# A fourth pair of seven products in the down projections of a two-layer decoder trunk, with own pages for sums of weights, an earlier table load and separate statistics tiles

## The chip, the cores and the metric

One core of one Trainium2 chip runs the whole kernel in one launch. The metric is the device time of that core in microseconds (us). Before the change the median of three runs was 2143.47 us (2143.34 to 2143.54).

## The reference

Input is x (256 tokens of 2048 features, float32) with the weights. Each sublayer is `h = h + RMSNorm_post(f(RMSNorm_pre(h)))`.

```python
def short_conv_mixer(u, w_in, conv_w, w_out):
    proj = u @ w_in
    xin, gate_c, gate_b = jnp.split(proj, 3, axis=-1)
...
    return (gate_b * conv) @ w_out
...
def sq_relu_mlp(u, w_up, w_down):
    return jnp.square(jax.nn.relu(u @ w_up)) @ w_down
```

Layer 0 is a gated convolution of width 3 over tokens and an MLP with 8192 hidden features. Then keys and values for layer 1 come from the normed h. Layer 1 is stick-breaking attention with 16 heads of 128, and again an MLP. Nearly all arithmetic is in the weight products: 2048 x 6144, 2048 x 2048, two MLPs of 2048 x 8192 and 8192 x 2048, keys and values 2048 x 4096, queries and output 2048 x 2048 each.

## The kernel before

**Split operands.** Every weight and every activation is split into a high part (rounded to the float32r format) and a low part (the rest), and a product is the sum of high x high, high x low and low x high. So one *product* (`product`, line 557) is three matmuls of 128 x 128 by 512 columns into one PSUM bank. ScalarE (ACT) makes the high part of a page of weights as a copy (line 389 in `act`), VectorE (DVE) the low part as a subtraction (line 397 in `tt`), both in `split` (line 487). TensorE (PE) multiplies.

**Groups.** A `Group` computes 256 tokens by 1024 columns from 2048 rows of weights, in sixteen chunks of 128 rows; a chunk of weights is a 512 KB page of 128 x 1024. For each chunk there are four products: two token blocks b by two column halves c, into four PSUM banks `acc`. Each MLP runs in four quarters q of 2048 hidden features. A quarter is two up groups (j = 0, 1), whose results go through relu, transpose and square into the operands `hid`, and two down groups, which read `hid` and gather into `part` pages. There are eight quarters in all.

**Pairs of seven.** Two chunks form a pair, that is a 2 x 2 block product with eight products. For the pairs in `UP_SEVEN` and `DN_SEVEN` (line 316, both pairs 0, 1 and 2) the method `seven` (line 610) uses seven products in place of eight, by Winograd's scheme: four sums of weight quarters t1 to t4 (DVE, 512 columns each), and sums of the activations, made once per pair and quarter by `make_forms` (line 529). Products go to three of the `acc` banks and to four banks q of the other set. `combine` (line 678) joins those four with DVE operations, and `finals` (line 688) adds them to the `acc` banks at the end of the group. The first up group of each layer and the last down group of each layer have no pairs of seven. `turns` (line 711) sets the sequence of the pairs: 3, 0, 4, 1, 5, 2, 6, 7 with the three pairs of seven between the others.

A seven takes three pages of class `raw` (two loaded, one for the sums t1 and t2) and one of `r2` (t4), and four pages each of `hi` and `lo`, the last one half used. t3 overwrites a quarter of the second raw page.

**The planner.** Nothing is ordered by hand on the engines. The code records tasks, and `Plan.place` (line 162) lays them out beforehand: each task has an engine, an estimated duration, a due time derived from the tasks that need it, and pages from pools of fixed size (`SLOTS`, line 29). An engine then runs its list strictly in that sequence. PE runs the products in the recorded sequence, with transposes and attention matmuls as side tasks between them. Loads go out on SyncE's queue (SP) once a raw page is free.

**Start.** ACT issues the load of the gains, then takes its first table together with the first split of x (`enter`, line 949). In the lead stage six PSUM banks are filled while x and the input weights arrive. A mean over features is a matmul with a matrix of 1/2048 (`mean`, line 344; `statistics`, line 964).

**Norms.** `Norms.post` (line 788) squares a finished bank on ACT with a running sum into one column of the tile `stats` (line 352, shared by all norms), multiplies by the gain on DVE (`mg`), and after the fourth quarter of columns adds up, takes the root on ACT and the reciprocal on DVE, and adds to h (`hh`). At four places the last group of a run ends in parts, so that this work begins earlier (`run` with `leave`, line 747): block 0 column half by column half, then block 1 with both halves together.

## Time and profile before

| | |
|---|---|
| median of 3 runs | 2143.47 us |
| profiled execution | 2144.19 us, span 2142.5 us |
| PE | 2121.9 us busy, 9942 matmuls |
| DVE | 1725.9 us, 2325 instructions |
| ACT | 1283.8 us, 1787 instructions |
| read from HBM | 417.40 MB, 199 GB/s over the span |
| a full MLP quarter | 169.52 us (up groups 43.28 each, down groups 41.48 each) |

The profile is of one execution. A row of the timeline gives start, length, engine, line, operation, written and read tiles, the count of merged instructions and, in brackets, how long the engine stood idle before and what released it. Lengths of following instructions on one engine may overlap. In the names, h and l before a letter are high and low part, r the raw page, and u, d, in the stage (up, down, input); a page of a pair of seven carries layer, quarter, group, pair and a letter: rd0201c is layer 0, quarter 2, down group 0, pair 1, page c, which holds the sums t1 and t2. Line numbers are those of the kernel before; in the changed one they are shifted by one in the helpers.

### The profile page before, as it was taken

What the parts mean: (1) busy time and instruction counts of PE and PEld (TensorE: products, weight loads), DVE (VectorE), ACT (ScalarE), POOL (GpSimd) and SP (SyncE); (2) the same over time, 40 slices, a digit from 0 to 9 for tenths busy, and PEclk for the clock granted to TensorE, in tenths of its full rate; (3) what the DMA queues carried; (4) which work ended last, traced back from release to release, by engine and by line L of the source; (5) the groups of instructions that cost most, each with busy time, mean ns of one, the idle gap of its engine ahead of it and who ended that gap; (6) DMA issues with size and microseconds to landing.
All of it is one profiled execution on the core that took longest, in us unless ns stands there. A gap on an engine that the chain in (4) does not pass through costs nothing.

```text
span 2142.5 us, 27458 instructions
## 1 busy us (share of the span) xinstructions
PE 2121.9 (99%) x9942; PEld 1773.0 (83%) x9942; DVE 1725.9 (81%) x2325; ACT 1283.8 (60%) x1787; POOL 1.0 (0%) x7
## 2 busy tenths in 40 slices
PE   8999999999999999999999999999999999999998
PEld 7888888788888888888888888888788888888886
DVE  7766656898999899899656777558988998999995
ACT  6444445765575566566557776547655665665663
POOL 0000000000000000000000000000000000000000
PEclk9999999999999999999999999999999999999999
DMA  8656666456556656667664446655566466656672
GB/s 314 186 189 187 208 226 205 158 197 207 195 178 219 204 175 207 216 198 264 221 207 151 158 158 198 228 190 191 171 217 205 165 222 208 195 196 201 189 277 103
DMA packets 118648, 427.59 MB, mean 200 GB/s; under 512 B 13168, under 2 KB 13296, under 8 KB 118512
## 3 DMA queue, kind: packets, MB, share of 16 engines
q1 hardware_dynamic: 118368, 425.77, 59.9%
q8 instruction: 78, 1.28, 0.2%
q14 instruction: 58, 0.48, 0.1%
q10 hardware_dynamic: 144, 0.07, 0.0%
HBM read 417.40 MB, written 8.39 MB: 199 GB/s over the span
## 4 chain that ended last, share of the span: by engine, by line
PE 99%; ACT 0%; DVE 0%; DMA 0%; issue 0%; DVEq 0%; ACTq 0%
PE acc L560 72%; PE acc L436 11%; PE q L560 11%; PE tr L443 2%; PE lead L436 2%; PE z L1193 0%; PE o L1243 0%; PE ex L1223 0%; PE o L1244 0%; PE z L1194 0%; DMA x<-xT 0%; ACT hid L389 0%; ACT hu L389 0%; DVE hh L404 0%; PE ey L1228 0%
## 5 line engine op out<-in xcount | busy, mean ns | idle before, releaser
L560 PE MATMUL acc<-hu,u 128*128 128x512 f32 x1376 | 439.7, 391 | 0.0
L560 PE MATMUL acc<-hd,hid 128*128 128x512 f32 x1376 | 435.4, 390 | 0.0
L560 PEld LDWEIGHTS acc<-hd,hid 128*128 128x128 f32 x1376 | 258.4, 188 | 53.0
L560 PEld LDWEIGHTS acc<-hu,u 128*128 128x128 f32 x1376 | 258.3, 188 | 52.7
L560 PE MATMUL acc<-lu,u 128*128 128x512 f32 x688 | 267.8, 389 | 0.0
L560 PE MATMUL acc<-ld,hid 128*128 128x512 f32 x688 | 267.8, 389 | 0.0
L397 DVE TENSOR_TENSOR ld<-rd,hd 128x1024 fp32r<-128x1024 f32 x172 | 208.1, 1222 | 51.3 <-ACT hd L389 49.7
L397 DVE TENSOR_TENSOR lu<-ru,hu 128x1024 fp32r<-128x1024 f32 x172 | 208.4, 1222 | 42.6 <-ACT hu L389 41.4
L389 ACT ACTIVATE hd<-rd 128x1024 fp32r<-128x1024 f32 x172 | 180.1, 1057 | 101.9 <-PE acc L560 73.8
L389 ACT ACTIVATE hu<-ru 128x1024 fp32r<-128x1024 f32 x172 | 178.8, 1059 | 84.3 <-PE acc L560 55.1
L397 DVE TENSOR_TENSOR lin<-rin,hin 128x1024 fp32r<-128x1024 f32 (+1 forms) x102 | 117.6, 1162 | 68.6 <-ACT hin L389 66.4
L389 ACT ACTIVATE hin<-rin 128x1024 fp32r<-128x1024 f32 (+1 forms) x102 | 102.0, 1009 | 116.5 <-PE acc L436 75.7
L436 PE MATMUL acc<-u,hin 128*128 128x512 f32 x672 | 168.5, 393 | 0.0
L560 PEld LDWEIGHTS acc<-ld,hid 128*128 128x128 f32 x688 | 129.2, 188 | 26.2
L560 PEld LDWEIGHTS acc<-lu,u 128*128 128x128 f32 x688 | 129.3, 188 | 25.9
L436 PEld LDWEIGHTS acc<-u,hin 128*128 128x128 f32 x672 | 120.9, 189 | 21.7
L436 PEld LDWEIGHTS acc<-u,lin 128*128 128x128 f32 x672 | 91.7, 190 | 6.6
L436 PE MATMUL acc<-u,lin 128*128 128x256 f32 x672 | 93.7, 282 | 0.0
L560 PE MATMUL acc<-hk,u 128*128 128x512 f32 x256 | 86.0, 398 | 0.0
L560 PE MATMUL acc<-hv,u 128*128 128x512 f32 x256 | 82.8, 394 | 0.0
L560 PE MATMUL acc<-hq,u 128*128 128x512 f32 x256 | 81.7, 393 | 0.0
L397 DVE TENSOR_TENSOR q<-q,q 128x512 f32<-128x512 f32 x112 | 76.8, 686 | 4.6
(3165 smaller groups left out, 4140.2 us busy)
## 6 DMA issues: line engine op xcount, KB each, us to landing
ru<-w_up SPq DMA_DIRECT2D x172, 512.0 KB, 3.8
rd<-w_dn SPq DMA_DIRECT2D x172, 512.0 KB, 4.4
rin<-w_in SPq DMA_DIRECT2D x94, 512.0 KB, 3.6
ro<-w_out SPq DMA_DIRECT2D x32, 512.0 KB, 3.5
rv<-w_v SPq DMA_DIRECT2D x32, 512.0 KB, 3.9
rk<-w_k SPq DMA_DIRECT2D x32, 512.0 KB, 4.4
rq<-w_q SPq DMA_DIRECT2D x32, 512.0 KB, 3.8
rwo<-w_wo SPq DMA_DIRECT2D x32, 512.0 KB, 3.5
```

What stands on the lines that cost most here:

```text
L389: nc.scalar.activation(out_.w(), in_.r(), func, scale=val(scale), **more)
L397: "DVE", dve(width(out_)), lambda: nc.vector.tensor_tensor(out_.w(), a.r(), b.r(), op=op),
L436: lambda: nc.tensor.matmul(out_.w(), lhsT.w(), rhs.w(), start=start, stop=stop, skip_group_check=skip),
L443: nc.tensor.matmul(to.w(), src.r(), ident.tile[:], is_transpose=True, start=j == 0, stop=True, skip_group_check=True)
L560: nc.tensor.matmul(ps.w(), a.w(), w.w(), start=first and j == 0, stop=last and j == 2, skip_group_check=skip)
```

## The change

`DN_SEVEN` gains pair 4, so each of the fourteen down groups with pairs of seven does four pairs with seven products and four with eight; `turns` then gives the sequence 3, 0, 5, 1, 2, 4, 6, 7. The page of t1 and t2 has its own class `rt`. The pools become 6 raw, 2 rt, 2 r2, 6 hi, 5 lo, 8 x8, 8 x4 and 12 c2. The planner now counts a read of a PSUM bank by another engine as something to wait for, and takes 0.08 us (DVE) or 0.09 us (ACT) off between following operations of an engine. ACT's table for the root is asked for as a task of its own at the start. `mean` is replaced by `ones` with the scale 1/2048 in the root. Every statistic has its own tile. The last groups of a run end half by half in both blocks. A branch that would make sums by DMA is rewritten, but stays unused (`SUMS_BY_DMA` is empty).

```diff
-SLOTS = {"raw": 8, "r2": 2, "hi": 6, "lo": 6, "x8": 8, "x4": 6, "c2": 14}
+SLOTS = {"raw": 6, "rt": 2, "r2": 2, "hi": 6, "lo": 5, "x8": 8, "x4": 8, "c2": 12}
...
+    OVERLAP = {"DVE": 0.08, "ACT": 0.09}
...
+            if b.bank is not None:
+                t.preds.update(w for a, z, w in b.reads if w.eng != eng and any(a < q and p < z for p, q in v.spans))
...
-                avail[e] = t.end
+                avail[e] = t.end - (self.OVERLAP.get(e, 0.0) if dur > 0.2 else 0.0)
...
-DN_SEVEN = (0, 1, 2)
+DN_SEVEN = (0, 1, 2, 4)
...
     def small(n=1):
-        a = used[0]
-        used[0] += n
-        return stats.col(a, a + n)
+        used[0] += 1
+        b = home([P, n], F32, f"stat{used[0]}")
+        b.home, b.owner = False, True
+        return b.col()
...
+    plan.task("ACT", 0.05, lambda: None, table=TABLES[AF.Sqrt])
...
-            r0, r1, r2 = [raw_page(f"r{self.name}{j}{z}") for z in "abc"]
-            r3 = page("r2", [P, HALF], F32, f"r{self.name}{j}d")
-            load(r0.col(), w[base], own=(r0, r1, r2))
+            r0, r2 = raw_page(f"r{name}a"), page("rt", [P, CW], F32, f"r{name}c")
...
+                r1 = raw_page(f"r{name}b")
+                r3 = page("r2", [P, HALF], F32, f"r{name}d")
+                load(r0.col(), w[base])
...
-            for c in range(2):
-                for i in range(gr.n - EDGE, gr.n):
-                    gr.half(0, c, i, i == gr.n - 1)
-                gr.finish(0, c)
-            for i in range(gr.n - EDGE, gr.n):
-                gr.unit(1, i, i == gr.n - 1)
-            for c in range(2):
-                gr.finish(1, c)
+            for b in range(NB):
+                for c in range(2):
+                    for i in range(gr.n - EDGE, gr.n):
+                        gr.half(b, c, i, i == gr.n - 1)
+                    gr.finish(b, c)
...
-            self.ss = [small(4) for _ in range(NB)]
+            self.ss = [[small() for _ in range(4)] for _ in range(NB)]
...
-            mm(ps.col(0, T), mean.col(), acc.col(0, T), 0.44)
-            act(rstd, ps.col(0, T), AF.Sqrt, bias=eps.col())
+            mm(ps.col(0, T), ones.col(), acc.col(0, T), 0.44)
+            act(rstd, ps.col(0, T), AF.Sqrt, bias=eps.col(), scale=1.0 / D)
```

What the planner makes of it is seen at three places. On DVE in layer 0, quarter 2, first down group, before the change (rd, hd and ld are raw, high and low pages of the down weights; 0201 and 0202 with a letter are pairs 1 and 2 of this group, 02010 and 02011 its chunks 10 and 11, which are pair 5, of eight; the number behind the underscore only tells buffers apart):

```order
L397 TENSOR_TENSOR ld0201c_7222<-rd0201c_7066,hd0201c_7210 128x1024
L397 TENSOR_TENSOR ld0201a_7237<-rd0201a_7064,hd0201a_7220 128x1024
L397 TENSOR_TENSOR ld0201b_7251<-rd0201b_7065,hd0201b_7232 128x1024
L397 TENSOR_TENSOR ld0201d_7263<-rd0201d_7185,hd0201d_7241 128x512
L397 TENSOR_TENSOR ld02010_7270<-rd02010_7137,hd02010_7246 128x1024
L397 TENSOR_TENSOR ld02011_7275<-rd02011_7163,hd02011_7258 128x1024
L397 TENSOR_TENSOR rd0202c_7229<-rd0202b_7228,rd0202a_7227 128x512
L397 TENSOR_TENSOR rd0202c_7229<-rd0202c_7229,rd0202a_7227 128x512
L397 TENSOR_TENSOR rd0202b_7228<-rd0202b_7228,rd0202a_7227 128x512
L397 TENSOR_TENSOR rd0202d_7301<-rd0202c_7229,rd0202b_7228 128x512
L397 TENSOR_TENSOR ld0202c_7308<-rd0202c_7229,hd0202c_7296 128x1024
L397 TENSOR_TENSOR ld0202a_7318<-rd0202a_7227,hd0202a_7306 128x1024
```

The same engine and group after the change, from the sums of pair 4 (rd0204) to its first split (here high and low pages carry a number for the letter: ld02022 is the third page of pair 2, ld02040 the first of pair 4; hid and hs4 are sums and low parts of hidden activations for pair 4):

```order
L398 TENSOR_TENSOR rd0204c_7385<-rd0204c_7385,rd0204a_7317 128x512
L398 TENSOR_TENSOR hid_7239<-hid_7239 128x128
L398 TENSOR_TENSOR ld02022_7417<-rd0202b_7262,hd02022_7402 128x1024
L398 TENSOR_TENSOR rd0202d_7422<-rd0202c_7356,rd0202b_7262 128x512
L398 TENSOR_TENSOR hid_7239<-hid_7239,hid_7226 128x128
L398 TENSOR_TENSOR rd0204b_7341<-rd0204b_7341,rd0204a_7317 128x512
L398 TENSOR_TENSOR hid_7226<-hid_7226,hid_7239 128x128
L398 TENSOR_TENSOR hid_7226<-hid_7226 128x128
L398 TENSOR_TENSOR ld02023_7443<-rd0202d_7422,hd02023_7432 128x512
L398 TENSOR_TENSOR rd0204d_7450<-rd0204c_7385,rd0204b_7341 128x512
L398 TENSOR_TENSOR ld02040_7458<-rd0204c_7385,hd02040_7436 128x1024
L398 TENSOR_TENSOR hs4_7448<-hid_7226,hs4_7448 128x256
```

Between the splits of pairs 1 and 2 there stood a pair of eight, ahead of the sums of pair 2; now pair 2 follows pair 1 directly, and the sums of pair 4 and the hidden sums stand among the splits of pair 2.

The second place is ACT at the first switch from an up group to the next (layer 0, quarter 0; relu reads a finished bank acc, tr is its transpose by PE, hu0018 and hu0019 are splits of the next group's weights). Before:

```order
L389 ACTIVATE hu0018_3757<-ru0018_3616 128x1024
L389 ACTIVATE hid_3765<-tr_3752 128x512
L389 ACTIVATE relu_3772<-acc01_3276 128x512
L389 ACTIVATE hid0_3743<-hid_3765 128x4x128
L389 ACTIVATE hu0019_3784<-ru0019_3628 128x1024
L389 ACTIVATE hid_3792<-tr_3778 128x512
L389 ACTIVATE relu_3796<-acc11_3364 128x512
L389 ACTIVATE hid1_3798<-hid_3792 128x4x128
L389 ACTIVATE hid_3812<-tr_3801 128x512
```

After:

```order
L390 ACTIVATE hid_3818<-tr_3808 128x512
L390 ACTIVATE relu_3823<-acc01_3332 128x512
L390 ACTIVATE hu0018_3827<-ru0018_3672 128x1024
L390 ACTIVATE hid0_3802<-hid_3818 128x4x128
L390 ACTIVATE hid_3841<-tr_3832 128x512
L390 ACTIVATE relu_3847<-acc11_3424 128x512
L390 ACTIVATE hid1_3850<-hid_3841 128x4x128
L390 ACTIVATE hu0019_3858<-ru0019_3690 128x1024
L390 ACTIVATE hid_3866<-tr_3860 128x512
```

The split hu0019 moved from ahead of the fourth relu to behind it, and hu0018 from ahead of the third relu to behind it. On PE twelve, twelve and three matmuls stood between the four transposes; now there are nine each time.

The third place is the start of ACT's list, with what each row waits for (DMAHW1 and DMAHW0 are the landings of the first page of x and the gains, DMAHW2 that of the first weights). Before and after:

```order
L457 DMA gv<-vecs 128x128
L389 ACT_TABLE_LOAD [waits DMAHW1_49]
L389 ACTIVATE u_115<-x,gv 128x256 [waits DMAHW0_49]
L389 ACTIVATE u_115<-x,gv 128x256
L389 ACTIVATE hin_119<-rin_81 128x256 [waits DMAHW2_49]
```

```order
L458 DMA gv<-vecs 128x128
L1368 ACT_TABLE_LOAD
L390 ACTIVATE u_175<-x,gv 128x256 [waits DMAHW1_49,DMAHW0_49]
L390 ACTIVATE u_175<-x,gv 128x256
L390 ACTIVATE hin_179<-rin_144 128x256 [waits DMAHW2_49]
```

The wait for x moved from the table load to the first split. Further down that list the last split of x (u) stood behind sixteen splits of weights and now stands behind thirteen.

## The prediction, made before the run

> **What bounds the kernel now.** I read the page's first part, then the waits of TensorE (PE), then one full quarter of an MLP in the table of windows, then the chain.

> ```profile
> PE 2121.9 (99%) x9942; PEld 1773.0 (83%) x9942; DVE 1725.9 (81%) x2325; ACT 1283.8 (60%) x1787; POOL 1.0 (0%) x7
> ```
> ```profile
> PE lead L436 <- ACT hin L389: 6.9, 1, 6.9
> PE tr L443 <- ACT relu L389: 2.0, 2, 1.0
> PE q L560 <- ACT hid L389: 1.4, 2, 0.7
> PE lead L436 <- DVE u L404: 1.3, 1, 1.3
> ```
> ```profile
> 787.36:956.88 169.52, 169.52 (x765) 140.66 (x765) 156.12 (x191) 104.08 (x131) 0.00 (x0) 1.00 0.61 199
> ```
> ```profile
> 1949.65 17.68 PE acc L560 x78
> ```

> PE is the bound: 2121.9 of 2142.5 us. Its waits come to 11.6 us, all in six places; the rest of the 20.6 is the tail behind its last matmul. In the quarter (columns: length, PE, PEld, DVE, ACT, POOL, clock, DMA share, GB/s) PE never stops, at full clock. So removed matmuls count one for one, as long as the Vector engine (DVE), which makes their operands, keeps up: it is busy 156.12 of 169.52. A product is three matmuls; 78 take 17.68 us, so 0.68 us a product.

> **The change part by part.**

> *The fourth pair of seven.* Fourteen down groups (seven in each layer) lose one product each: 14 x 0.68 = 9.52 us off PE. What it adds to DVE needs DVE's pace, start to start:

> ```profile
> 925.19 1.89 DVE L397 TENSOR_TENSOR q<-acc,q 128x512 f32<-128x512 f32 x3 [0.67 <-PE acc L560]
> ...
> 946.21 1.48 DVE L397 TENSOR_TENSOR hid<-hid 128x128 f32<-128x128 f32 x5
> 947.60 1.22 DVE L397 TENSOR_TENSOR lu0312c<-ru0312c,hu0312c 128x1024 fp32r<-128x1024 f32 x1
> 948.74 2.10 DVE L397 TENSOR_TENSOR hs<-hid,hs 128x256 fp32r<-128x256 f32 x6
> 950.75 0.69 DVE L397 TENSOR_TENSOR ru0312b<-ru0312b,ru0312a 128x512 f32<-128x512 f32 x1
> ```
> ```profile
> 963.91 1.22 DVE L397 TENSOR_TENSOR ld<-rd,hd 128x1024 fp32r<-128x1024 f32 x1
> 967.12 2.73 DVE L397 TENSOR_TENSOR q<-acc,q 128x512 f32<-128x512 f32 x4 [1.99 <-PE acc L560]
> ...
> 983.08 1.23 DVE L397 TENSOR_TENSOR ld0301c<-rd0301c,hd0301c 128x1024 fp32r<-128x1024 f32 x1
> 984.22 0.69 DVE L397 TENSOR_TENSOR rd0301b<-rd0301b,rd0301a 128x512 f32<-128x512 f32 x1
> 984.82 1.23 DVE L397 TENSOR_TENSOR ld0301a<-rd0301a,hd0301a 128x1024 fp32r<-128x1024 f32 x1
> ```

> A 1024-wide operation is followed 1.14 us after its start (983.08 to 984.22), though one lasts 1.23; a 512-wide one 0.60 after (984.22 to 984.82); five of 128 columns take 1.39 (0.28 each), six of 256 take 2.01 (0.34 each). A pair as eight needs two 1024-wide splits: 2.28. As seven it needs three of them, one of 512 and four sums of 512: 3.42 + 0.60 + 2.40 = 6.42. So 4.14 more a pair, 8.28 for a quarter's two down groups, and the combinations of the hidden rows for the new pair add 4 x 0.28 + 2 x 0.34 = 1.80. DVE: 156.12 + 10.08 = 166.2 in a quarter in which PE has 169.52 - 1.36 = 168.16. It fits on average, by 1.2%. ScalarE (ACT) gets one and a half splits more a pair:

> ```profile
> L389 ACT ACTIVATE hd<-rd 128x1024 fp32r<-128x1024 f32 x172 | 180.1, 1057 | 101.9 <-PE acc L560 73.8 <-issue 18.6 <-PE q L560 3.3
> ```

> 3.2 us a quarter on 104.08, and two copies of forms: it has room, and it waited mostly for PE to free a page.

> The average does not settle it, because the pairs now run 3, 0, 5, 1, 2, 4, 6, 7 with three sevens in a row, each 4.76 us on PE and 6.42 on DVE. The tightest point is pair 4 of a quarter's first down group.

> ```profile
> 968.73 0.39 PE L560 MATMUL acc<-hu,u 128*128 128x512 f32 x1
> ```
> ```profile
> 413.41 0.44 PE tr L443 x4
> ...
> 419.86 1.06 ACT hu L389
> 420.92 0.48 ACT hid L389
> ...
> 421.94 0.67 PE tr L443 x4
> 422.63 0.61 ACT hid L389
> ...
> 423.28 2.79 PE q L560 x6
> ```

> Let T be PE's end with the up group before it, 969.1 by its last matmul. PE reaches pair 4 at T + 5.44 (pair 3) + 4 x 0.44 (transposes) + 4.76 + 5.44 + 4.76 + 4.76 = T + 26.9. DVE's last step for the up group ended at 969.85, T + 0.8. From there to the first split of pair 4 the changed order has eleven 1024-wide operations (12.5), fifteen sums and half splits (9.0), four of the hidden rows (2.4) and four of 128 (1.1): T + 25.8, and two forms that the same product reads, T + 26.5. The lead is 0.4 us. The trace shows what a crowded stretch loses: from 925.19 to the end of 963.91's pace (965.05) DVE worked 39.86 us on operations that by these paces make 39.3, 1.5% off; over 25 us that is 0.4. So PE waits about 0 to 0.5 there. In the second group no transposes and no hidden rows lie between, and the lead is about 1. Bounds: nothing lost, or 1 us in each of fourteen groups. I take **2 us**, near the lower end, as the stretch quoted lost 0.6 us.

> *Pools.* The sums' first page leaves "raw" for "rt", so a seven takes two raw pages for three, and six hold three sevens. The five fewer pages of raw, lo and c2 cost nothing while PE is not waiting for a load, and it waits for none; if that cover goes, it shows as the same DVE wait, which the 2 us and its bounds hold. Separate tiles for statistics add no operation.

> *ScalarE's table.*

> ```profile
> 1.24 1.37 SPq L422 DMA_DIRECT2D rin<-w_in  x3
> ...
> 4.33 1.28 ACT L389 ACT_TABLE_LOAD   x1 [4.33 <-DMA x<-xT]
> 5.62 0.91 ACT L389 ACTIVATE u<-x,gv 128x256 fp32r<-128x256 f32 x2
> ...
> 6.44 1.32 ACT L389 ACTIVATE hin<-rin 128x256 fp32r<-128x256 f32 x4
> ...
> 6.89 2.93 PE L436 MATMUL lead<-u,hin 128*128 128x512 f32 x6 [6.89 <-ACT hin L389]
> ```
> ```profile
> rin<-w_in SPq DMA_DIRECT2D x1, 256.0 KB, 3.8
> ```

> The load sat behind the wait for x and in front of the first split. Without that wait it runs while x is on its way: 1.28 us. What is late next is the first half page of weights, 1.24 + 3.8 = 5.04, still before ACT would want it (4.33 + 0.9 = 5.2). So **1.28**, at least 0 if later loads, which land one behind the other, set the pace instead.

> *The last operand of the lead stage.*

> ```profile
> 36.57 1.06 ACT L389 ACTIVATE hin<-rin 128x1024 fp32r<-128x1024 f32 x1 [2.22 <-PE lead L436]
> 37.53 0.90 ACT L389 ACTIVATE u<-x,gv 128x256 fp32r<-128x256 f32 x2
> ```

> PE waited 1.3 us for u, because u stood on ACT behind the sixteenth split, which waited for PE. In the changed order it stands behind the thirteenth: **1.3** gone, bounds 0 and 1.3.

> *The first switch from up group to up group, once in each layer.* The fourth relu stood behind a split that had waited for PE (419.86), and PE's transpose behind the relu: twice 1.0. Now PE has nine matmuls (2.04 us) between two transposes, and the relu stands one split earlier: **2.0** gone. The wait for hid (1.4) stays, since a split stands ahead of that copy now. Behind the first such stop the clock fell:

> ```profile
> 423.46:426.87 3.41, 3.41 (x9) 2.67 (x10) 2.53 (x6) 2.11 (x4) 0.00 (x0) 0.50 0.00 0
> 1502.40:1505.80 3.40, 3.40 (x15) 2.81 (x16) 2.83 (x7) 3.30 (x6) 0.00 (x0) 1.00 0.00 0
> ```

> Nine matmuls for fifteen in the same time: 6 x 0.227 = 1.36 us. It fell at one of two like places, so the row alone gives half of it after any such stop; with one of the two waits gone I take all of **1.36**. [...]

> *The tail.*

> ```profile
> 2132.81 0.69 ACT L389 ACTIVATE dump<-acc,stats 128x512 f32<-128x512 f32 x1 [3.59 <-PE acc L560]
> ...
> 2135.13 0.69 ACT L389 ACTIVATE dump<-acc,stats 128x512 f32<-128x512 f32 x1 [1.54 <-DVE stats L397]
> ```
> ```profile
> 2133.62 1.41 DVE L404 SCALAR_TENSOR_TENSOR mg<-acc,stats,gpost 128x512 f32<-128x512 f32 x2 [1.10 <-ACT dump L389]
> ...
> 2136.47 2.74 DVE L404 SCALAR_TENSOR_TENSOR hh<-mg,stats,hh 128x512 f32<-128x512 f32 x4
> ```
> ```profile
> 2133.06 0.39 PE L560 MATMUL acc<-hd,hid 128*128 128x512 f32 x1
> ```

> The last square waited for a sum in the one statistics tile. With its own tile, and the quarter (1, 0) finished four products earlier, it starts at PE's end, 2133.45; mg 0.81 behind it (2132.81 to 2133.62), 0.75 long, then the reciprocal: hh starts at 2135.2 for 2136.47. I take **1.2**, bounds 0 and 1.7. The same reordering at the three other ends of groups hides behind the next group's products; no PE wait is there now. If that cover is short, up to 1 us each.

> Sum: -9.52 + 2.0 - 1.28 - 1.3 - 2.0 - 1.36 - 1.2 = -14.7. The profiled execution took 2144.19 (span 2142.5 and 1.7 around it), 0.7 above the median 2143.47: 2129.5 in its terms, **2128.8** for the median.

> **The rivals.** *Slower: DVE loses the row of sevens.* If DVE comes w late to pair 4 in each of the fourteen groups, the time is 2143.47 - 16.7 + 14w. From w = 1.2 the gain is gone, from 1.5 it is slower. At w = 1.8: 2152.0. For it: room of 1.2%, a lead of 0.4 us, one lo page fewer. Against: in the quoted stretch, as crowded, DVE came 2 us early to 967.12. At w = 0.7 it is 2136.6, the milder form.

> *Slower: no operation starts before the last has ended.* The quarter's 191 operations by their full lengths (76 of 1.22, 100 of 0.69, the small ones 5.4) make 167 us, more than the 156.12 measured, so this is nearly excluded. With the additions it would be 178.6, 9.1 above today's 169.52, in seven quarters' worth 64 us: about 2200. [...]

> *The edits outside the MLP don't pay.* Loads and ACT hold the first stage anyway, the relu chain finds another split to stand behind, the tail stays: -9.52 + 2.0 = 2136.0. For it: the early loads land in turn; against: each has one named wait.

> **How the numbers follow.** Forecast (2124 to 2133) 0.60; milder late DVE (2133 to 2141, 0.04 of it above 2139) 0.19; edits not paying 0.10; losses that cancel the gain (2139 to 2148) 0.05; slower 0.05; full lengths 0.01. Everything hidden and the hid waits gone as well would give 2125.4; the range goes to 2124 below, and to 2139 above, where it takes in the two milder cases. About 0.2% (4.3 us) is what a measurement can tell: faster 0.85, within 0.09, slower 0.06.

> **What would show it.** PE's waits: no u, no relu; hid near 1.4; a new line "acc or q behind DVE ld" of about 2 us, over 10 if the rival holds. A full quarter of 168.2 to 169 us with DVE near 166. First matmul at 5.6; no half clock near 423; from PE's end to the span's end 7.8 in place of 9.0. I am wrong if the quarter stays at 169.5 or above.

## The result and the profile after

The changed kernel took 2130.02 us (median of 4 runs, 2129.72 to 2130.78), the kernel before 2143.51 in the same comparison (2143.34 to 2143.67): 0.9938 of it, 95% interval 0.992 to 0.9955. The forecast was 2128.8, in a range of 2124 to 2139. The profiled execution took 2130.27 us, with a span of 2128.55 for 2142.47.

The page's first part and the waits of TensorE (us in total, times, longest), kernel after:

```profile
PE 2111.5 (99%) x9900; PEld 1764.5 (83%) x9900; DVE 1770.7 (83%) x2456; ACT 1307.8 (61%) x1830; POOL 1.0 (0%) x7
```
```profile
PE lead L437 <- ACT hin L390: 5.9, 1, 5.9
PE q L563 <- ACT hid L390: 1.4, 2, 0.7
PE tr L444 <- DVE mg L398: 1.0, 2, 0.5
PE acc L563 <- DVE lv L405: 0.6, 2, 0.3
```

42 matmuls are gone (14 products of three). The waits for u and relu are gone, hid stays as foretold, and two new lines stand there: transposes behind `mg`, and products of the values behind `lv`. The line that was forecast, products behind DVE's `ld`, is missing. From 9.70 us to PE's end at 2120.50 the granted clock is 1.00. Layer 0, quarter 2, from its first up product to that of quarter 3 (length, PE, PEld, DVE, ACT, POOL, clock, DMA share, GB/s):

```profile
707.61:875.78 168.17, 168.17 (x759) 139.61 (x758) 162.58 (x210) 107.92 (x136) 0.00 (x0) 1.00 0.61 200
```

That is 1.35 us less than 169.52: two products, in full. DVE is busy 6.5 us longer than before, not 10.1. The start and the end of the timeline:

```profile
1.23 1.28 ACT L1368 ACT_TABLE_LOAD   x1 [1.23 <-PEq L1434]
4.62 0.91 ACT L390 ACTIVATE u<-x,gv 128x256 fp32r<-128x256 f32 x2 [2.10 <-DMA gv<-vecs]
5.88 0.79 PE L437 MATMUL lead<-u,hin 128*128 128x512 f32 x1 [5.88 <-ACT hin L390]
```
```profile
2120.11 0.39 PE L563 MATMUL acc<-hd,hid 128*128 128x512 f32 x1
2120.59 0.69 ACT L390 ACTIVATE dump<-acc,stat 128x512 f32<-128x512 f32 x1 [2.00 <-PE acc L563]
2122.26 2.74 DVE L405 SCALAR_TENSOR_TENSOR hh<-mg,stat,hh 128x512 f32<-128x512 f32 x4
```

The table loads while x is on its way, but what is late next are the gains gv, not the weights: the first matmul comes 1.01 us earlier. Behind PE's last matmul 8.05 us are left (2120.50 to 2128.55) for 9.02.

A ledger from the first and last matmul of every stage in both traces (after minus before, change within the stage):

| stage | forecast | measured |
|---|---|---|
| first matmul (table) | -1.28 | -1.01 |
| lead stage (u) | -1.3 | -1.44 |
| fourteen down groups, products | -9.52 | -9.52 (0.68 each) |
| the same, DVE late | +2.0 | 0 |
| second up groups (relu and clock) | -3.36 | -3.97 (2.78 and 1.19) |
| three ends of groups inside | 0, "up to 1 us each" | +2.95 (0.99, 0.94, 1.02) |
| tail | -1.2 | -0.97 |
| sum | -14.7 | -13.96, span -13.92 |

### The profile page after: what moved, and what is told of

It reads as the page before. It is cut to its first block, busy times and chain, and to the rows that moved or that the text cites. A ratio compares the mean times of both kernels' runs of the same rounds, so it can differ in the third digit from the quotient of the medians.

```text
span 2128.5 us, 28143 instructions
## 1 busy us (share of the span) xinstructions
PE 2111.5 (99%) x9900; PEld 1764.5 (83%) x9900; DVE 1770.7 (83%) x2456; ACT 1307.8 (61%) x1830; POOL 1.0 (0%) x7
## 3 DMA queue, kind: packets, MB, share of 16 engines
q8 instruction: 77, 1.26, 0.2%
## 4 chain that ended last, share of the span: by engine, by line
PE 98%; DVE 1%; ACT 1%; issue 0%; DMA 0%; DVEq 0%; ACTq 0%
PE acc L563 69%; PE q L563 12%; PE acc L437 11%; PE tr L444 2%; PE lead L437 2%; PE o L1264 0%; PE z L1214 0%; DVE hh L405 0%; DVE lv L405 0%; ACT hid L390 0%; DVE lu L398 0%; DMA gv<-vecs 0%; ACT hu L390 0%; PE ex L1244 0%; PE o L1265 0%
## 5 line engine op out<-in xcount | busy, mean ns | idle before, releaser
L563 PE MATMUL acc<-hu,u 128*128 128x512 f32 x1544 | 493.1, 392 | 0.0
L563 PEld LDWEIGHTS acc<-hu,u 128*128 128x128 f32 x1544 | 289.7, 188 | 59.6 <-DVE u L405 0.8
L563 PE MATMUL acc<-lu,u 128*128 128x512 f32 x772 | 300.9, 390 | 0.0
L398 DVE TENSOR_TENSOR ld<-rd,hd 128x1024 fp32r<-128x1024 f32 x144 | 174.0, 1220 | 24.3 <-PE acc L563 23.9
L390 ACT ACTIVATE hd<-rd 128x1024 fp32r<-128x1024 f32 x144 | 148.3, 1054 | 55.9 <-PE acc L563 40.0
L563 PEld LDWEIGHTS acc<-lu,u 128*128 128x128 f32 x772 | 145.1, 188 | 28.9
L563 PEld LDWEIGHTS acc<-ld,hid 128*128 128x128 f32 x688 | 129.3, 188 | 26.1
L563 PE MATMUL q<-hd,hs 128*128 128x512 f32 x336 | 121.8, 390 | 0.0
L563 PE MATMUL q<-hu,us 128*128 128x512 f32 x252 | 91.9, 391 | 1.4 <-ACT hid L390 1.4
```

Source lines behind the costliest of these rows:

```text
L390: nc.scalar.activation(out_.w(), in_.r(), func, scale=val(scale), **more)
L398: "DVE", dve(width(out_)), lambda: nc.vector.tensor_tensor(out_.w(), a.r(), b.r(), op=op),
L563: nc.tensor.matmul(ps.w(), a.w(), w.w(), start=first and j == 0, stop=last and j == 2, skip_group_check=skip)
```

## The experiments

First theory: the seven pays in full since DVE stays just ahead; the small edits give 7.4 us and lose 3 again at the three ends. The rivals are written into each expectation. The kernel before took 2143.5 to 2144.5 (median) in the five comparisons, so kernels are compared by ratio or by the span of the profiled run (2128.5 for the changed one). Kernels that don't differ in the lead stage differed there by -0.5 to +1.0 us; effects below 1 us are therefore read as shifts within a stage.

| run | median, us | ratio to before, 95% | span |
|---|---|---|---|
| three sevens (e1) | 2140.01 | 0.9977 (0.9968 to 0.9986) | 2137.7 |
| the seven on the kernel before (e2) | 2168.38 | 1.011 (1.0096 to 1.0124) | 2166.2 |
| old ends inside (e3) | 2131.51 | 0.9937 (0.9925 to 0.9949) | 2129.7 |
| low half twice (e4) | 2139.29 | 0.9976 (0.9966 to 0.9985) | 2139.4 |
| no OVERLAP (e5) | 2164.88 | 1.0097 (1.0083 to 1.011) | 2162.4 |
| shared pages (e6) | 2140.53 | 0.9983 (0.9974 to 0.9991) | 2139.4 |
| OVERLAP on e2 (e7) | 2142.53 | 0.9992 (0.9984 to 1.0001) | 2140.8 |
| no bank rule (e8) | 2132.86 | 0.9946 (0.9932 to 0.9959) | 2131.6 |
| three sevens, no OVERLAP (e9) | 2144.43 | 0.9997 (0.9989 to 1.0006) | 2142.8 |
| later transposes, fifth pair (e10) | 2172.64 | 1.0134 (1.012 to 1.0148) | 2170.6 |
| late table, one tile (e11) | 2131.3 | 0.9941 (0.9928 to 0.9955) | 2130.9 |
| copies sooner (e12) | 2131.06 | 0.9936 (0.9922 to 0.9949) | 2128.9 |

**e1, the fourth pair undone.**

```diff
-DN_SEVEN = (0, 1, 2, 4)
+DN_SEVEN = (0, 1, 2)
```

> The changed kernel with DN_SEVEN back at (0, 1, 2): the fourth pair alone undone, every other edit kept. Theory (the seven saves its product in full, because VectorE stays just ahead of TensorE): 14 products of 0.68 us come back, +9.5, so 2139.5 us, between 2139.0 and 2140.0. Rival (part of the saving is lost to VectorE, and the small edits carry more than they seem to): the fourth pair is worth 7.5 or less, so 2137.5 or below.

The median is at the upper end of the theory's range, the span 9.2 us longer, and every one of the fourteen groups by 0.68. The same quarter in this run:

```profile
709.83:879.37 169.54, 169.54 (x766) 140.69 (x765) 154.73 (x191) 105.46 (x130) 0.00 (x0) 1.00 0.62 199
```

So inside the changed kernel the fourth pair is worth its products in full, with 7.85 us more of DVE in the quarter.

**e2, the pair on the kernel before.**

```diff
-SLOTS = {"raw": 8, "r2": 2, "hi": 6, "lo": 6, "x8": 8, "x4": 6, "c2": 14}
+SLOTS = {"raw": 8, "r2": 2, "hi": 6, "lo": 5, "x8": 8, "x4": 8, "c2": 12}
-DN_SEVEN = (0, 1, 2)
+DN_SEVEN = (0, 1, 2, 4)
```

> The kernel before with DN_SEVEN = (0, 1, 2, 4) and the counts of three pools changed (lo 5, x4 8, c2 12; the forms of a fourth pair need the x4 pages), without own pages for the sums, without the planner's two new rules, the early table, the split statistics and the new order of the ends. Theory (the pages, the planner and the pools are worth nothing here): 2143.5 - 9.5 = 2134.0 us, between 2133.3 and 2134.7. Rival (with the sums in shared pages of 8 the fourth seven waits for pages and loses its lead): 0.5 us or more lost in each of 14 groups, so 2141 or above.

Slower than before by 1.1%: in the range of the rival named, but far beyond its bound of 2141. The largest of TensorE's waits on DVE, and the quarter:

```profile
PE acc L560 <- DVE ld L397: 5.0, 8, 0.8
```
```profile
717.21:889.77 172.56, 170.09 (x760) 139.17 (x758) 164.47 (x209) 106.18 (x136) 0.00 (x0) 1.00 0.59 195
```

The quarter got 3.0 us longer than before, although two products left it: the prediction's first rival, DVE losing the row of sevens. Of the 4.4 us lost in this quarter 2.5 show as idle time of PE; the rest stands in matmul rows that last longer (170.09 us busy for 168.17 in the changed kernel). The losses lie in the eight first down groups, not in all fourteen: from each layer's second quarter on they are 3.7 to 5.0 us longer than before, in the first quarter 1.4; the second groups are 0.68 shorter, as planned. Own pages, planner and the rest are thus worth 38 us of span (2166.2 to 2128.5) with the pair, where the theory had nothing.

**e5, e6, e7 and e9: pages or planner?** e5 takes the planner's overlap away, e6 the own pages, e7 adds the overlap to e2, e9 takes pair and overlap away together.

```diff
-    OVERLAP = {"DVE": 0.08, "ACT": 0.09}
+    OVERLAP = {}
```

> The changed kernel without OVERLAP in the planner (it counts VectorE's and ScalarE's operations end to end again), all else kept. The run of the seven on the kernel before lost 3.7 to 5.7 us in each of seven first down groups, with TensorE waiting for VectorE. Theory P (what it lacked was the own pages for the sums): this kernel has them, so no loss, 2129.3 to 2131.5 us. Theory O (what it lacked was the planner's new idea of VectorE's time, which orders the sums): most of that loss comes back, 2140 or above.

```diff
-SLOTS = {"raw": 6, "rt": 2, "r2": 2, "hi": 6, "lo": 5, "x8": 8, "x4": 8, "c2": 12}
+SLOTS = {"raw": 8, "r2": 2, "hi": 6, "lo": 5, "x8": 8, "x4": 8, "c2": 12}
...
-            r0, r2 = raw_page(f"r{name}a"), page("rt", [P, CW], F32, f"r{name}c")
+            r0, r2 = raw_page(f"r{name}a"), raw_page(f"r{name}c")
...
-                load(r0.col(), w[base])
+                load(r0.col(), w[base], own=(r0, r1, r2))
```

> The changed kernel with the sums t1 and t2 back in a page of the raw pool (8 pages, claimed three at a time by the first load of a pair, as before), the same memory in all; planner's rules, early table, statistics and ends kept. Theory P (the shared pages make loads and sums of a pair come late): a loss of 2 us or more in each of eight first down groups, 2146 us or above. Theory O (the planner's idea of time): no loss, 2129.3 to 2132.

```diff
+    OVERLAP = {"DVE": 0.08, "ACT": 0.09}
...
-                avail[e] = t.end
+                avail[e] = t.end - (self.OVERLAP.get(e, 0.0) if dur > 0.2 else 0.0)
```

> The kernel of the seven on the kernel before (three pools changed) with OVERLAP alone added to its planner. Theory P: the loss stays, 2164 us or above. Theory O: the loss goes, 2134 to 2140 us.

```diff
-    OVERLAP = {"DVE": 0.08, "ACT": 0.09}
+    OVERLAP = {}
-DN_SEVEN = (0, 1, 2, 4)
+DN_SEVEN = (0, 1, 2)
```

> The changed kernel with DN_SEVEN = (0, 1, 2) and without OVERLAP: the fourth cell of a table of two by two (with both 2130.0 us in its own comparison, without the fourth pair 2140.0, without OVERLAP 2164.9). Theory I (the planner's idea of VectorE's time only matters when the fourth pair brings VectorE near TensorE's time): the loss of 34 us in the first down groups isn't there, and only the waits for relu come back, 2140.0 + 2.4 = 2142.4 us, between 2141 and 2144. Rival (OVERLAP is worth the same with three pairs): 2140.0 + 34.9 = 2174.9.

Each theory got part of it; e6 and e7 end between the ranges given for them. Without the overlap: 34 us, the larger share. Without own pages: 11 us, of which 8.8 are 1.10 us in each of the eight first down groups; of the rest 1.3 is the wait for u, below. The overlap on e2 brings its span from 2166.2 to 2140.8. What a first group loses against the changed kernel is 4.4 to 5.7 us in e2 (2.1 in the first quarters) and 1.1 in e7, as much as the shared pages cost in e6. And e9 is 5.1 us above e1 in span, not 34: the overlap matters for the down groups only with the fourth pair. (e9's median lies 2 us above the forecast for it, and 0.4 above its range.) TensorE's waits in e5 and in e6:

```profile
PE acc L563 <- DVE ld L398: 14.2, 22, 0.8
...
PE tr L444 <- ACT relu L390: 2.0, 2, 1.0
```
```profile
PE acc L563 <- DVE ld L398: 6.1, 8, 0.8
...
PE lead L437 <- DVE u L405: 1.3, 1, 1.3
```

What does a planner's number do on the chip? DVE just ahead of the first down group of quarter 1, in e5 (the group starts at 629.73) and in the changed kernel (625.42):

```profile
627.10 2.73 DVE L398 TENSOR_TENSOR q<-acc,q 128x512 f32<-128x512 f32 x4 [1.29 <-PE acc L563]
629.75 0.68 DVE L398 TENSOR_TENSOR rd0100c<-rd0100c,rd0100a 128x512 f32<-128x512 f32 x1
```
```profile
618.94 0.68 DVE L398 TENSOR_TENSOR rd0100c<-rd0100c,rd0100a 128x512 f32<-128x512 f32 x1
...
621.09 1.22 DVE L398 TENSOR_TENSOR ld<-rd0100c,hd 128x1024 fp32r<-128x1024 f32 x1 [0.26 <-ACT hd L390]
622.35 2.73 DVE L398 TENSOR_TENSOR q<-acc,q 128x512 f32<-128x512 f32 x4
625.00 1.22 DVE L398 TENSOR_TENSOR ld<-rd0100a,hd 128x1024 fp32r<-128x1024 f32 x1
```

In e5 the finals (q<-acc,q) stand ahead of the sums of pair 0, and DVE idles 1.29 us for PE's last product while those sums could have been made. In the changed kernel the second and third sums, t4 and the first low page are done before the finals, without a wait: some 3 us more in store at the start of the row of sevens. A likely reason: a planner that counts operations end to end believes DVE later than it is, thinks that PE will be done by then, and puts the finals first. That is read from the two orders; the planner's own times are not shown here. In e6 the fault is a single one near pair 4 (DVE, then PE):

```profile
657.39 0.69 DVE L398 TENSOR_TENSOR q<-q,q 128x512 f32<-128x512 f32 x1 [0.89 <-ACT q L390]
658.00 0.68 DVE L398 TENSOR_TENSOR ld<-rd0104d,hd 128x512 fp32r<-128x512 f32 x1
```
```profile
660.47 0.51 PE L563 MATMUL acc<-ld,hid 128*128 128x512 f32 x1 [0.77 <-DVE ld L398]
```

The last half page of pair 4 stands behind a combination that waits for ACT's copy. Why that order comes out of shared pages was not followed further.

**e4, the lead measured.** The low half of the first page of pair 4 is made twice:

```diff
                     done[r] = split(r, f"{name}{len(done)}", 0, r.shape[1])
+                    if r is r2 and self.name[0] == "d" and j == 4:
+                        low = plan.tasks[-1]
+                        low.fn = lambda once=low.fn: (once(), once())
```

> The changed kernel in which VectorE works out the low half of the first page of pair 4 twice in each of the 14 down groups (the same result twice, 1.13 us more of VectorE at that place, nothing reordered). In the trace the next page of that pair comes 0.46 us ahead of its first matmul in 6 of the groups and 0.68 in two; in the other six 1.44 to 1.71. Theory (this lead is all that keeps TensorE from waiting, and it is refilled by the next pair 4): waits of 0.67 in six groups, 0.45 in two, none in six, +4.9, so 2134.9 us, between 2134.0 and 2136.2. Rival A (VectorE has spare time at that place that the lead doesn't show): no change, 2129.6 to 2130.5. Rival B (VectorE is already the bound of the down groups): 14 x 1.13 = +15.8, so 2145.8.

Between the theory and rival B, outside the ranges of both: 9.9 us in the fourteen groups (a further 1.0 arose in the lead stage). DVE and PE in quarter 1, first group:

```profile
652.18 2.48 DVE L398 TENSOR_TENSOR ld<-rd0104c,hd 128x1024 fp32r<-128x1024 f32 x2
654.57 0.75 DVE L398 TENSOR_TENSOR hs<-hid,hs 128x256 fp32r<-128x256 f32 x2
...
658.12 2.35 DVE L398 TENSOR_TENSOR ld<-rd,hd 128x1024 fp32r<-128x1024 f32 x2
```
```profile
654.71 0.49 PE L563 MATMUL q<-ld,hs 128*128 128x512 f32 x1 [0.25 <-DVE ld L398]
655.38 0.73 PE L563 MATMUL q<-hd,hs 128*128 128x512 f32 x2 [0.18 <-DVE hs L398]
```

What is tight is not the next page but the forms hs, which stand behind the doubled operation. They came 1.26 us later (2.48 for one step of 1.22). Six first groups lost 1.0 us each, the two of quarter 0 0.79, five second groups 0.21 to 0.25 and one 1.14: some 0.25 us were to spare in a first group, 1.0 in a second. The spare time is about as thin as the leads forecast (0.4 and about 1), and TensorE waited once it was used up (0.25 and 0.18 us in these rows).

**e10, a fifth pair, and later transposes.**

```diff
-                    lat += 0.35
+                    lat += 1.8
...
-        return DN_SEVEN if (q, j) != (QUARTERS - 1, 1) else ()
+        return (DN_SEVEN + (5,) if j else DN_SEVEN) if (q, j) != (QUARTERS - 1, 1) else ()
```

> The changed kernel with two additions in different places. (a) The planner takes 1.8 us in place of 0.35 from VectorE's or ScalarE's end to a transposition on TensorE; at the output projection's end this puts the eight transposes of hh three products (0.68 us) later into the row of products. Theory (they stall there since the planner believes VectorE 0.9 us earlier than it is): the stalls of 0.9 to 1.0 us at three ends become 0.3 or less each, -2. Rival: they move to other transposes, 0. (b) A fifth pair of seven, (0, 1, 2, 4, 5), in the six second down groups alone. Running a low half twice showed 1.0 us to spare there. Theory (one pair more asks 3.3 us more of VectorE than of TensorE's 4.8 in the time of the group, and VectorE is at 162.5 of 168.2 in a quarter): the six products come off in full, -4.1, and the whole at 2124.0 us, between 2123 and 2126. Rival (the first down group of the next quarter or this one falls behind VectorE, as in the run of the seven on the kernel before): 0.5 us or more per quarter lost, 2127 or above.

Both failed. The second down groups got 3.1 us longer instead of 0.68 shorter, and DVE, busy 167.25 us in layer 0's quarter 2, is what PE waits for:

```profile
722.11:894.88 172.77, 169.83 (x757) 138.44 (x756) 167.25 (x218) 109.16 (x141) 0.00 (x0) 1.00 0.59 195
```

The first down groups got longer too, and so did the first two up groups of each layer. The later transposes made waits elsewhere: relu 3.6 us for none, hid 3.7 for 1.4. Both additions change the order of one stream, and (a) moves every transposition in it; how much of the 42 us is the fifth pair's alone was not separated.

```profile
PE q L563 <- DVE ld L398: 10.4, 19, 0.8
...
PE q L563 <- ACT hid L390: 3.7, 2, 1.9
...
PE tr L444 <- ACT relu L390: 3.6, 2, 1.8
```

**e3, e8 and e12: the 3 us at the ends inside.** e3 puts the old order of the last eight products back at these three ends; e8 drops the planner's rule on bank reads; e12 makes ScalarE's copies due earlier.

```diff
...
+            if leave == "end":
...
+            else:
+                for i in range(gr.n - EDGE, gr.n):
+                    gr.unit(1, i, i == gr.n - 1)
+                for c in range(2):
+                    gr.finish(1, c)
...
-                run([gr], leave=leave)
+                run([gr], leave=("end" if after.last else True) if leave else False)
```

> The changed kernel with the old order of the last eight products at the three ends inside the program (output projection, first layer's last down group, second output projection) and the new order at the program's end alone. Theory (the new order brings VectorE two evictions earlier than before, ahead of the work that the transposes of the first half wait for, and that costs 1 us at each of the three): -3 us, so 2127.0 us, between 2126.5 and 2127.8. Rival (the stall of these ends comes from the planner's new rules, which order the tasks there, or from the smaller pools): no change, 2129.6 to 2130.4.

```diff
-            if b.bank is not None:
-                t.preds.update(w for a, z, w in b.reads if w.eng != eng and any(a < q and p < z for p, q in v.spans))
```

> The changed kernel without the planner's rule on two engines that read one PSUM bank, all else kept. Theory (the 1 us lost at each of the three ends inside comes from where the planner happens to put two evictions among the additions to the stream, and any change of its rules or pools shuffles it): between 2128 and 2131 us, the stall at those ends of some other length or on another operation. Rival (the rule itself makes these stalls, by keeping VectorE's eviction behind ScalarE's): all three go, 2127.0 to 2127.8.

```diff
-                    act(self.raw[b, c].col(k % 4 * P, (k % 4 + 1) * P), src, AF.Copy, scale=g(self.gain, k), soon=20.0)
+                    act(self.raw[b, c].col(k % 4 * P, (k % 4 + 1) * P), src, AF.Copy, scale=g(self.gain, k), soon=2.0)
```

> The changed kernel with one number changed: the due time of ScalarE's copies uraw at the entry of an MLP, 2 us in place of 20 us behind their place in the program. Pages of a pool are handed out in the program's order, and these copies take a c2 page ahead of the last two evictions mg of the group before; so a late copy holds the page of an mg, and the transposes wait for mg, since they write its bank. Theory: with early copies the stalls of 0.9 us at the output projection's end and at the second one's go, the one before the values (which has no such copies) stays; -1.6 to -1.9, so 2128.3 us, between 2127.8 and 2129.0. Rival (VectorE is simply full there and is late whatever the pages): no change, 2129.6 to 2130.5.

The theories of e3 and e12 fell, and so did e8's rival. With the old order the three ends lose 0.2 to 0.3 us more each, with `hh` for `mg` as the thing waited for; without the bank rule two of them lose 1.05 more, and the whole lies 1.9 us above the range given; with early copies the wait for `mg` goes, others come in its place, and the two entries of an MLP (the ends of the two output projections) lose 0.3 us more. TensorE's waits, in e3, e8 and e12:

```profile
PE tr L444 <- DVE hh L405: 1.9, 2, 0.9
```
```profile
PE tr L442 <- DVE hh L403: 1.6, 2, 0.8
...
PE tr L442 <- DVE mg L396: 1.2, 2, 0.6
```
```profile
PE tr L444 <- DVE u L405: 0.7, 2, 0.4
...
PE acc L563 <- DVE lu L398: 0.4, 2, 0.2
```

DVE is full there: from 2 us before the first up group of layer 0 to 6 us behind its start it is busy 7.93 of 8.00 us, in the kernel before, in the changed one and in e2 alike, but only 3.8 of the 6 us ahead of that. So whatever comes first, something else is late, and an operation done ahead is time gained. (In the changed kernel ACT is nearly full there too, 7.94 us for 6.96 before; in e2, which loses as much, it is busy 7.10.) The best pointer is e2: it has the old ends, the old planner and the one statistics tile, and yet the first up group of layer 0, which no pair of seven precedes, loses 1.19 us against the kernel before. Up to there only the pools differ. DVE ahead of that group, before and in e2 (it starts at 366.52 and 366.08):

```profile
353.73 1.23 DVE L397 TENSOR_TENSOR lu<-ru,hu 128x1024 fp32r<-128x1024 f32 x1 [1.49 <-ACT hu L389]
356.45 1.23 DVE L397 TENSOR_TENSOR lu<-ru,hu 128x1024 fp32r<-128x1024 f32 x1 [1.49 <-ACT hu L389]
365.03 1.22 DVE L397 TENSOR_TENSOR lu<-ru,hu 128x1024 fp32r<-128x1024 f32 x1
```
```profile
354.74 1.22 DVE L397 TENSOR_TENSOR lu<-ru,hu 128x1024 fp32r<-128x1024 f32 x1 [1.50 <-PE acc L560]
364.58 1.22 DVE L397 TENSOR_TENSOR lu<-ru,hu 128x1024 fp32r<-128x1024 f32 x1
```

With six low pages DVE has made two of the group's low halves 8.8 us and more before it starts; with five, one, and it waited for PE where before it waited for ACT's high half: PE is what frees a low page. One 1024-wide step is 1.14 us, about what each end loses. Every kernel with the smaller pools has one low half fewer ahead at the two entries of an MLP, and loses 0.97 us or more at each, with three pairs (e1) as with four. That the pools do it there is shown by e2; that it is `lo` (and not x4 or c2) is argued from these rows. At the values the order counts as well: e7, with the same pools and the same low half missing, loses 0.2 us there, where the changed kernel loses 0.94. A kernel with six low pages and four pairs was not run.

**e11, table and statistics undone.** `stats` is one tile again, and the task that asks for the table is out:

```diff
-    plan.task("ACT", 0.05, lambda: None, table=TABLES[AF.Sqrt])
...
+    stats = home([P, 256], F32, "stats")
```

> The changed kernel with two of its small edits undone, which act in different places: ScalarE's table loaded behind the first x again, and all norm statistics in one tile again. Theory: +1.0 us at TensorE's first matmul (5.88 to 6.9), and +1.0 between TensorE's last matmul and the span's end (8.0 to 9.0): 2132.0 us, between 2131.5 and 2133.0. Rival (with one tile other operations on statistics are ordered behind each other too, so ends inside lose as well): 2134 or above.

The first matmul is 0.86 us later, near the 1.0. The tail does not change, and the whole lies 0.2 us below the range given. Its last matmul and hh:

```profile
2122.43 0.39 PE L564 MATMUL acc<-hd,hid 128*128 128x512 f32 x1
...
2124.59 2.74 DVE L407 SCALAR_TENSOR_TENSOR hh<-mg,stats,hh 128x512 f32<-128x512 f32 x4
```

8.04 us from PE's end to the span's end, for 8.05. So the separate tiles are worth nothing that shows. The tail is 7.8 to 8.05 us in every run with the new order at the program's end (without the pair, the overlap, the own pages or the bank rule as well) and 9.0 in e2 and e7, which have the old one. So the shorter tail comes from finishing the quarter (1, 0) four products earlier.

No kernel tried beats the changed one; e12 and e3 are level with it (0.9936 and 0.9937 for 0.9938).

## Why the prediction held, and where its steps did not

**The products.** 14 x 0.68 came off to the hundredth (ledger, e1).

**DVE late to pair 4, +2.0.** Nothing was lost, but not because of the lead that the prediction counted. DVE and PE at pair 4 of quarter 1, first group, in the changed kernel:

```profile
650.41 0.75 DVE L398 TENSOR_TENSOR hs<-hid,hs 128x256 fp32r<-128x256 f32 x2
```
```profile
651.16 0.39 PE L563 MATMUL q<-hd,hs 128*128 128x512 f32 x1
...
651.62 0.62 PE L563 MATMUL q<-hd,hs 128*128 128x512 f32 x2
```

The row from 625.00 to the end of the forms holds the operations that were counted. By their paces they make 25.7 us; they took 26.1, so the crowded stretch lost about the 0.4 us put down for it, and the forms end at 651.16, just when PE reaches the pair. The step that failed is the point to which the lead was measured: the low forms are read by the product's third matmul (651.62), 0.45 us after its first. That is what e4 found as some 0.25 us to spare, and in the changed kernel this thin lead cost nothing (0 in the ledger).

**DVE's load, +10.1 a quarter.** It was 6.5. The additions are 11.7 us by their full lengths (167.6 to 179.3 in the quarter). But before, 142 of the quarter's 191 operations started before the last had ended, which took 11.4 us off; now 189 of 210 do, and it takes off 16.7. The forecast counted the overlap of the new operations, and not that the old ones would overlap more as well.

**Pools and planner at nothing.** This was the weak step: their price was put at nothing. That was true only of the order that the changed kernel comes with, on which the lead was counted. The pair, the own pages and the overlap are one edit: without the overlap the same pair costs 34 us, without the own pages 11. The first rival, with its mechanism, is what e2 and e5 do, in the first down groups; its chance of 0.05 to be slower holds for this order alone, not for the pair.

**The ends inside, "hides; if that cover is short, up to 1 us each".** They cost 2.95 us, the full bound, but not by the order of the ends (e3). What the step missed is what the smaller pools do there, most likely that five low pages in place of six take away a low half that DVE had made ahead. It stood under "pools", priced at nothing since PE waited for no load; the page of a product's low half is filled by DVE, not by a load.

**The table, -1.28.** -1.01: the mechanism was right, the next late thing was another, gv.

**u, -1.3.** -1.44. Right; and e6 shows where it comes from: with eight raw pages the wait of 1.3 us is back (in e2 and e7 it is there too), so six pages let fewer splits stand ahead of u.

**relu and clock, -3.36.** -3.97: 1.19 for a relu stop, by the layer whose clock had not fallen, and 1.58 for the clock, by the difference of the layers; the forecast had 1.0 and 1.36. In e5 and e9 the relu waits are back, in e7 they are gone: the planner's overlap moves the split hu0019.

**Tail, -1.2.** -0.97, by one of the two reasons given (e11).

The errors nearly cancelled: 2.0 too careful in the down groups, 2.95 too bold at the ends, and four small ones. That the sum came within 0.8 us is in part luck.

## What to carry to other kernels

Where a planner writes the order, its durations are part of the kernel: an error of 0.08 us an operation cost 34 us here as soon as an engine came within 4% of the bound. Price a pool by the engine that fills its pages, not by loads alone, and count at each change of stage how many operations were made ahead. When an edit raises the load of the second engine, find the one place of least lead and measure it by doubling an operation there; totals over a quarter did not tell a kernel that gains from one that loses: the quarter in the changed kernel has DVE busy for 162.6 us, in e2, 24 us slower than before, for 164.5.

## What the runs showed of the hardware

**The half clock, as granted.** The stretches at half clock in the table of windows, in e9, e10 and e2 (in e2 inside first down groups, with PE's rows ahead of the first):

```profile
1502.95:1506.36 3.41, 3.41 (x9) 2.63 (x9) 2.30 (x3) 1.88 (x5) 0.00 (x0) 0.50 0.20 36
```
```profile
425.96:429.38 3.42, 3.42 (x10) 2.67 (x9) 2.75 (x4) 1.88 (x2) 0.00 (x0) 0.50 0.18 20
1521.64:1525.06 3.42, 3.42 (x9) 2.65 (x9) 2.30 (x3) 1.27 (x3) 0.00 (x0) 0.50 0.12 20
```
```profile
1921.46:1924.87 3.41, 3.41 (x8) 2.75 (x9) 2.75 (x3) 0.33 (x2) 0.00 (x0) 0.50 0.39 120
2095.54:2098.95 3.41, 3.41 (x10) 2.63 (x9) 2.48 (x3) 0.60 (x1) 0.00 (x0) 0.50 0.99 345
```
```profile
1919.59 0.50 PE L560 MATMUL acc<-ld1202d,hid 128*128 128x512 f32 x1 [0.81 <-DVE ld1202d L397]
...
1920.72 0.50 PE L560 MATMUL q<-ld1204c,hs 128*128 128x512 f32 x1 [0.17 <-DVE ld1204c L397]
...
1921.39 1.19 PE L560 MATMUL q<-hd1204c,hs 128*128 128x512 f32 x2 [0.17 <-DVE hs L397]
```

Of the same two stops in both layers (relu 0.98 us, hid 0.69) one pair was followed by it in each of three kernels: that of layer 0 before and in e5, that of layer 1 in e9. In e10 it followed the pair of both layers, 1.78 and 1.86 us there. In e2, which also has a relu stop of 1.0 us and a hid stop of 0.7 in each layer, the two stretches lie at first down groups, behind stops of 0.81, 0.17 and 0.17 us (0.82, 0.17 and 0.17 at the second). So in these runs the length of the stops does not tell behind which of them the clock falls, and what does was not shown: nothing was run to shift the stops.

**A doubled operation on one page.** In e4 two writes of one page took 2.48 us (652.18), where two of different pages took 2.35 (658.12).
